# Norm and turn of a gated delta rule's outputs, chunk by chunk, in a one-core decoder layer

## The chip, the cores and the metric

The kernel runs on one core of a Trainium2 chip. A core has a matrix engine (TensorE, PE in the profile), a vector engine (VectorE, DVE), an activation engine (ScalarE, ACT), a general engine (GpSimd, POOL) and a queue from which most transfers are issued (SyncE, SP). Each works through its own instructions in order, and semaphores make one wait for another. The metric is the time of one execution in device microseconds; lower is better. Several runs are taken, and one further execution is profiled.

## What is computed

One layer of a hybrid decoder over 1024 tokens of width 1024, in float32. Four heads of a gated DeltaNet and eight heads of dilated attention share one input and one output projection; a gated MLP with a short convolution follows. The part that matters here:

```python
def step(state, xs):                       # one chunk of the delta rule, head by head
    uv, wk, qd, at, ke, ge = xs
    u = uv - wk @ state
    o = qd @ state + at @ u
    state = ge * state + ke.T @ u
    return state, o
...
o_a = gated_delta_rule(qa, ka, va, g, beta)
o_a = rmsnorm(o_a, gdn_norm_w) * silu(z)   # per head: over its 128 features, then gated
...
x = x + concat(o_a, o_b) @ w_out           # o_b: dilated attention (softmax)
h = rmsnorm(x, norm2_w)
u = causal_dwconv(h @ w_up, ffn_conv_w)
x = x + (silu(gate) * up) @ w_down
```

## The kernel before

All products run on PE. Large ones are split in a high and a low part (`whi`, `wlo` for weights, `xhi`, `xlo` for the input) and done as three products of 128 by 512 (`mm3`); a product of 128 by 512 takes one issue slot of about 0.23 us. Nearly every instruction is recorded through a helper, so the profile shows line L193 for products, L140 for other instructions and L142 for those with high priority; tiles tell them apart.

The order on PE is written by a class called `Weave`. Generators (streams) for the dense projection, for the preparation of each head, for the chain of each head and for attention yield the time until they can go on; `run` takes the ready stream of lowest level. `Weave` keeps an estimate of when each engine is free and each tile ready. The dense projection has the highest level number, so its products fill what is left. The other engines' instructions get their order from a scheduler that follows priorities, and each engine keeps that order on the chip.

The stretch in question is the **chain**. For each of four heads and eight chunks of 128 tokens, `chain` issues:

- product of the keys `kT` with the state `ct`; DVE forms the residual `r` from it;
- product of the triangular inverse (called `um` in the trace) with `r`; DVE scales it to `wke`, ACT copies it to `w`;
- product of `ktok` with `wke`; DVE adds it to the decayed state, `ct`;
- two output products with `qat` (queries and attention weights), `ct` and `w`; ACT copies the second scaled by `rq` to `vtok`, DVE adds the first;
- ACT squares the chunk of `vtok` into `osq` and sums each row into a column of `ms` (an activation, and an instruction that reads the accumulator).

When a head's eight chunks are done, DVE turns `ms` into a mean, POOL raises it to the power −0.5 (`rsqrt`, one instruction for eight columns) and multiplies the whole of `vtok` (128 by 1024) by it. A stream `finish` turns the head with four 32-by-32 block transposes on DVE into a tile `ft` and stores it in device memory (`mixer[h]`, 512 KB). `ft` takes its buffer in the ring `kT*` of large tiles. Later the dense columns of kind `z` read it back as `og` and gate it.

Beside the chain, the dense stream works through `DENSE`, a list of columns of 128 features. For each, `weight` splits the next column's weights on ACT (`whi`) and DVE (`wlo`), 1024 elements per partition in one instruction each, and DVE evicts the products of each half (for attention's columns as `aqkv`). Attention begins behind the chain: scores, a DVE pass that masks and takes the maximum (`mx`), exponentials on ACT (`sm`), a reciprocal and a scaling on DVE, and transposes on PE (`ident,sm`).

ACT needs a table for its functions. The last SiLU before the chain is that of the values of head 3 (`vT`); the next exponential is that of the first softmax. Among POOL's other work in this stretch are memsets of `pb` tiles for attention. `mark` is a one-column constant tile, and the ring `t2` has two small buffers in all, which `w1` of the merges before the chain and `oT` of attention also use.

Of the kernel before, what the change touches and what calls it, by code (L numbers as in the profile page):

```python
# [15 lines left out]
P = 128  # L16
S = 1024
KT = 8
# [23 lines left out]
FSLACK = 0.5  # L42
DENSE = ([("k", 3), ("a", 0, 0), ("a", 0, 1)] + [(c, h) for h in range(4) for c in "qv"] + [("a", 0, 2)]
         + [("a", p, i) for p in (1, 2, 3) for i in range(3)] + [("z", h) for h in range(4)])


class Weave:
# [98 lines left out]
def hybrid_layer(tc, I, out):  # L146
# [72 lines left out]

    lows_made = []  # L220

    def weight(src, n=1024, st=None):
        if st is None:
            st = raw_weight(src, n)
        hi = tile_(wp, [P, n], F32R, "whi", "whi", 2)
        lo = tile_(wp, [P, n], F32R, "wlo", "wlo", 2)
        lows_made.append(split(st, hi, lo))
        return hi, lo

    def wk(src, st=None):  # L230
        return [t.rearrange("p (k m) -> p k m", k=KT) for t in weight(src, st=st)]

    n1 = const("n1", [P, KT])
    sa.dma_start(n1, I["n1"])
# [5 lines left out]
    def rsqrt(dst, src, n):  # L240
        po_.tensor_tensor(dst, src, mhalf[:, :n], op=OP.pow)
# [221 lines left out]
    def conv_silu(xr, j, name, tag):  # L463
        y = A(name, tag)
        ac.activation(y, xr, AF.Copy, scale=gcw[:, j, 3:4])
        for d in (1, 2, 3):
            inst = ve.scalar_tensor_tensor(y[:, d:], xr[:, :S - d], gcw[:, j, 3 - d:4 - d], y[:, d:],
                                           op0=OP.mult, op1=OP.add)
            if j // 4 == 1 and d == 2 and klast:
                after(inst, klast[-1], "the keys before go first")  # L470
        if j // 4 != 1:
            ac.activation(y, y, AF.Silu)
            return y

        th = ac.activation(xr, y, AF.Tanh, scale=0.5)
        klast.append(ve.scalar_tensor_tensor(y, xr, 1.0, y, op0=OP.add, op1=OP.mult))
        kends[j - 4] = th, klast[-1]
        return y
# [35 lines left out]
    def dense():  # L514

        yield from wv.until("first")
        yield from wv.until("norms")
        wv.add(2, first_keys())

        raw = [raw_weight(I["wi"][0])]  # L520
        nxt = wk(None, raw.pop())
        raw.append(raw_weight(I["wi"][1]))
        for i, col in enumerate(DENSE):
            kind, h = col[:2]
            if kind == "z":
                yield from wv.until(("o", h))
            w = nxt
            if i + 1 < len(DENSE):
                nxt = wk(None, raw.pop())
            if i + 2 < len(DENSE):  # L530
                raw.append(raw_weight(I["wi"][i + 2]))
            pair = []
            for hh in range(2):
                pt = bank("hf")
                yield wv.need(pt, *w)
                for k in range(KT):
                    mm3(pt, [t[:, k, :] for t in w], [t[:, half(hh)] for t in xs[k]], k == 0, k == KT - 1)
                    yield 0.0

                pair.append(pt)  # L540
                if hh == 0:
                    while put_off:
                        gate(*put_off.pop(0))
                    xr = A("aqkv" if kind == "a" else "xr", "go" if kind == "k" else "ev")
                if kind == "z":
                    ve.tensor_tensor(by_row(xr)[:, :, 4 * hh:4 * hh + 4], by_token(pt), by_token(rstdB[:, half(hh)]), op=OP.mult)
                else:
                    scaled(pair, "xr", kind == "a", t=xr, hs=(hh,))
            if kind == "k":
                T["k", h] = conv_silu(xr, 4 + h, "kT", "kT*")  # L550
                wv.add(3, kprep(h))
            elif kind == "q":
                q = conv_silu(xr, h, "qT", "qa")
                wv.add(4, qprep(h, q))
            elif kind == "v":
                v = conv_silu(xr, 8 + h, "vT", "qa")
                wv.add(4, vprep(h, v))
            elif kind == "z":
                og = gated[h] = A("og", "kT*")
                for b in range(4):  # L560
                    sq_.dma_start(og[32 * b:32 * b + 32].rearrange("j (a y) -> j a y", a=4),
                                 mixer[h].rearrange("(a j) (b y) -> b j a y", a=4, b=4)[b])
                if i + 1 < len(DENSE):
                    put_off.append((og, xr))
                else:
                    gate(og, xr)
            else:
                if col[2] < 2:
                    sy.dma_start(apark[h, col[2]], xr)
                else:  # L570
                    t = A("avt", "ev")
                    ve.transpose(t.rearrange("p (c n j) -> p n c j", c=4, n=NCH), by_block(xr))
                    for b in range(4):
                        sq_.dma_start(avdram[h].rearrange("u x (b j) -> b u x j", b=4)[b],
                                     t[32 * b:32 * b + 32].rearrange("u (x j) -> u x j", j=32))
                wv.done.add(col)
        wv.done.add("dense")
# [232 lines left out]
    def chain(h):  # L810
# [14 lines left out]
        for c in range(NCH):  # L825
            cs = slice(c * P, (c + 1) * P)
            if c == 2 and h < 2:
                qb = chain_load(h, 1)
            if c == 3 and h >= 2:
                yield from wv.until(("c", h - 2, 3))  # L830
                qb = chain_load(h, 1)
            if c == 4:
                qa = qb
            qT, at = [qa[:, i, (c % 4) * P:(c % 4 + 1) * P] for i in range(2)]
            if c == 0:
                r = vtok[:, cs]
# [12 lines left out]
            ua.activation(w, ps[:, P:2 * P], AF.Copy)  # L849
            if c < NCH - 1:  # L850
                yield wv.need(wke, slack=HOP)
                mm(ps[:, 2 * P:3 * P], ktok[:, cs], wke, 0.215)
                sn = sts[:, c % 2, :]
                if c == 0:
                    uv.tensor_copy(sn, ps[:, 2 * P:3 * P])
                else:
                    uv.scalar_tensor_tensor(sn, st, ge[:, c:c + 1], ps[:, 2 * P:3 * P], op0=OP.mult, op1=OP.add)
            yield wv.need(w, qa, slack=HOP)
            po = yield from next_bank("atr")
            if c:  # L860
                mm(po[:, P:2 * P], qT, st, 0.215)
            mm(po[:, :P], at, w, 0.215)

            ua.activation(vtok[:, cs], po[:, :P], AF.Copy, scale=rq[:, c:c + 1])
            if c:
                uv.scalar_tensor_tensor(vtok[:, cs], po[:, P:2 * P], gq[:, c:c + 1], vtok[:, cs], op0=OP.mult,
                                        op1=OP.add)
            if c < NCH - 1:
                st = sn
            osq = tile_(sp, [P, P], F32, "osq", "osq", 1)  # L870
            ua.activation(osq, vtok[:, cs], AF.Square, accum_out=ms[:, c:c + 1])
            wv.done.add(("c", h, c))

        uv.tensor_scalar(ms, ms, 1.0 / 128, EPS, op0=OP.mult, op1=OP.add)
        rsqrt(ms, ms, NCH)
        po_.tensor_tensor(v8(vtok), v8(vtok), ms[:, :, None].to_broadcast([P, NCH, P]), op=OP.mult)
        wv.add(1, finish(h, vtok))

    def finish(h, osb):
        yield wv.need(osb, slack=FSLACK)  # L880
        t = A("ft", "kT*")
        by_feature, src = t.rearrange("p (b c i) -> p b c i", b=4, c=NCH), osb.rearrange("p (c b j) -> p b c j", c=NCH, b=4)
        for b in range(4):
            ve.transpose(by_feature[:, b], src[:, b])
            yield 0.4
        sy.dma_start(mixer[h], t)
        wv.done.add(("o", h))


# [882 lines left out]
```

## Time and profile before

| | |
|---|---|
| Median of 3 runs | 1201.64 us (1201.17 to 1201.66) |
| Profiled execution, its own time | 1199.71 us |
| Its span (first to last instruction) | 1197.9 us |
| Granted TensorE clock over the span | 0.998 |
| Stretch of the chain in the span | about 225 to 292 us |
| First softmax | about 293 to 298 us |

Lines of a timeline give start and duration in us, engine, line, operation, output tile, input tiles, shapes and, in brackets, how long the engine sat idle before it and what released it. Lines of a group give busy time, mean duration in ns, and idle time before. Lines of waits give who waited for whom: total us, number of times, longest us. Lines of transfers give a count, a size and the median us from issue to landing. In a table of stretches each engine has its busy us and, in brackets, its number of instructions, in the order PE, PE's weight loads, DVE, ACT, POOL; the granted clock, the transfers' share and GB/s follow. DVE, ACT and PE pipeline, so the next instruction can start before the one before it has ended.

### The profile page before, as it was taken

How to read it: one execution, taken by the hardware profiler on the slowest of the kernel's cores; microseconds unless marked ns; L12 is line 12 of the kernel's file. 1: busy time of each engine (PE TensorE's matmuls, PEld its weight loads, DVE VectorE, ACT ScalarE, POOL GpSimd, SP SyncE). 2: the span in 40 equal slices, each digit the busy share in tenths (PEclk: the TensorE clock that was granted, in tenths of full speed). 3: DMA queues.
4: the chain of work that ended last, by engine and by line, in shares of the span. 5: the costliest groups of instructions: out<-in, count | busy, mean ns of one | idle time of the engine just before them, and what ended most of it. 6: DMA issues, size and time to landing. Idle time of an engine off the chain costs nothing.

```text
span 1197.9 us, 18219 instructions
## 1 busy us (share of the span) xinstructions
PE 1184.3 (99%) x6994; PEld 979.5 (82%) x6994; DVE 967.5 (81%) x1552; ACT 566.4 (47%) x1113; POOL 54.3 (5%) x50
## 2 busy tenths in 40 slices
PE   9999999998999999999999999999999999999997
PEld 7888888897777777888888888888888888888887
DVE  7686985586766687777898888989888889898987
ACT  7383344363433344555454544445444453445452
POOL 0212110023000000000000000000000000000001
PEclk9999999999999999999999999999999999999999
DMA  7423235536643314443222223131222396356724
GB/s 237 106 75 103 78 118 131 150 114 189 185 100 128 98 37 142 148 158 106 77 70 99 88 71 106 53 106 59 100 89 69 105 378 211 119 181 218 240 99 155
DMA packets 98600, 152.72 MB, mean 127 GB/s; under 512 B 37936, under 2 KB 51024, under 8 KB 98512
## 3 DMA queue, kind: packets, MB, share of 16 engines
q1 hardware_dynamic: 97792, 151.02, 39.4%
q8 instruction: 55, 0.90, 0.3%
q10 hardware_dynamic: 720, 0.53, 0.1%
q14 instruction: 33, 0.27, 0.1%
HBM read 115.59 MB, written 35.93 MB: 126 GB/s over the span
## 4 chain that ended last, share of the span: by engine, by line
PE 95%; DVE 2%; ACT 1%; issue 1%; DMA 1%; POOL 0%; DVEq 0%; ACTq 0%; POOLq 0%
PE ps L193 46%; PE pa L193 20%; PE dw L193 17%; PE pc L193 10%; PE ps L197 1%; PE ps L202 1%; DMA wst<-in_wu 1%; ACT sm L142 0%; PE warm L193 0%; DVE x1h L140 0%; DVE sm L142 0%; DVE aqkv L140 0%; DVE T L140 0%; ACT L142 0%; DVE wst L140 0%
## 5 line engine op out<-in xcount | busy, mean ns | idle before, releaser
L193 PE MATMUL dw<-pr 128*128 128x512 f32 (+1 forms) x984 | 211.4, 376 | 0.0
L193 PEld LDWEIGHTS dw<-pr 128*128 128x128 f32 x984 | 176.7, 188 | 33.7
L193 PE MATMUL ps<-xhi,whi 128*128 128x512 f32 x448 | 184.4, 412 | 0.0
L193 PE MATMUL ps<-xhi,wlo 128*128 128x512 f32 x448 | 175.2, 391 | 0.0
L193 PE MATMUL ps<-xlo,whi 128*128 128x512 f32 x448 | 174.8, 390 | 0.0
L193 PE MATMUL pa<-T,pair 128*128 128x512 f32 x528 | 127.1, 390 | 0.5 <-ACT u L140 0.5
L193 PEld LDWEIGHTS pa<-T,pair 128*128 128x128 f32 x528 | 98.9, 188 | 21.5 <-ACT u L140 1.0
L193 PEld LDWEIGHTS ps<-xhi,whi 128*128 128x128 f32 x448 | 84.3, 188 | 19.3 <-issue 2.7
L193 PEld LDWEIGHTS ps<-xhi,wlo 128*128 128x128 f32 x448 | 84.1, 188 | 18.5
L193 PEld LDWEIGHTS ps<-xlo,whi 128*128 128x128 f32 x448 | 84.4, 188 | 14.3
L140 ACT ACTIVATE u<-pa 128x512 f32<-128x512 f32 x44 | 26.3, 598 | 109.7 <-PE pa L193 109.7
L140 DVE SCALAR_TENSOR_TENSOR y<-xu,fcw,y 128x1023 f32<-128x1023 f32 (+1 forms) x44 | 56.4, 1281 | 24.4 <-ACT y L140 24.4
L140 ACT ACTIVATE whi<-wst 128x1024 fp32r<-128x1024 f32 (+2 forms) x38 | 38.5, 1014 | 68.8 <-PE ps L193 61.6
L140 ACT ACTIVATE pr<-wd 128x1024 fp32r<-128x1024 f32 x33 | 35.0, 1061 | 74.6 <-DVE wd L140 37.2
L193 PE MATMUL pa<-B,A 128*128 128x512 f32 x264 | 63.5, 389 | 0.0
L193 PE MATMUL pa<-T,S 128*128 128x512 f32 x264 | 63.4, 389 | 0.0
L193 PE MATMUL pc<-T,S 128*128 128x512 f32 x264 | 63.4, 389 | 0.0
L193 PE MATMUL pc<-B,pair 128*128 128x512 f32 x264 | 63.4, 389 | 0.0
L140 DVE TENSOR_TENSOR wst<-wst 128x512 f32<-128x512 f32 x88 | 60.4, 686 | 0.8
L193 PE MATMUL ps<-B,pair 128*128 128x512 f32 x252 | 60.5, 389 | 0.0
L142 ACT ACTIVATE sm<-sm,mx 128x128 f32<-128x128 f32 (+7 forms) x64 | 35.5, 555 | 50.3 <-DVE mx L142 50.3
L193 PEld LDWEIGHTS pc<-T,S 128*128 128x128 f32 x264 | 49.5, 188 | 10.3
(242 smaller groups left out, 2234.2 us busy)
## 6 DMA issues: line engine op xcount, KB each, us to landing
wst<-in_wu SPq DMA_DIRECT2D x44, 512.0 KB, 3.6
wd<-in_wd SPq DMA_DIRECT2D x44, 512.0 KB, 4.5
wst<-in_wi SPq DMA_DIRECT2D x25, 512.0 KB, 3.6
upark<-y SPq DMA_DIRECT2D x22, 512.0 KB, 3.5
r<-upark SPq DMA_DIRECT2D x22, 512.0 KB, 10.1
wa<-in_wd SPq DMA_DIRECT2D x22, 256.0 KB, 2.9
apark<-aqkv SPq DMA_DIRECT2D x8, 512.0 KB, 2.7
wst<-in_wo SPq DMA_DIRECT2D x8, 512.0 KB, 3.8
```

The lines of the kernel that those rows point to most:

```text
L140: return getattr(eng, op)(*a, **kw)
L142: return getattr(eng, op)(*a, **kw)
L193: tc.stamp_issue_order_token(nc.tensor.matmul(dst, lhs, rhs, start=start, stop=stop, **kw).ins, TOKEN)
L197: tc.stamp_issue_order_token(nc.tensor.transpose(dst, src, ident).ins, TOKEN)
L202: tc.stamp_issue_order_token(nc.tensor.transpose(dst, src[rows], ident[rows, rows]).ins, TOKEN)
```

## The change

- The mean square comes out of the square itself (a scale of 128^−0.5). Behind each chunk's square POOL adds the epsilon and takes the power for that one column.
- ACT multiplies each chunk by its column (`normed`), one chunk behind; the large multiply on POOL and the late instruction on DVE are gone.
- Two halves of a head are turned apart (`half_turned`), the first behind chunk 4, the second in `finish`, each with two transposes and a store of 256 KB of its own, in packets of 512 bytes. The half tiles are in the ring `t2`.
- The weights of three dense columns (`CHAINED`) are split in two halves of 512.
- One exponential of a column is ordered behind the last SiLU, and writes `mark`.

```diff
+CHAINED = [("a", 1, 1), ("a", 1, 2), ("a", 2, 0)]
...
-    def weight(src, n=1024, st=None):
+    def weight(src, n=1024, st=None, parts=1):
...
-        lows_made.append(split(st, hi, lo))
+        for i in range(parts):
+            sl = slice(i * n // parts, (i + 1) * n // parts)
+            low = split(st[:, sl], hi[:, sl], lo[:, sl])
+        lows_made.append(low)
...
-            ac.activation(y, y, AF.Silu)
+            last["silu"] = ac.activation(y, y, AF.Silu)
...
-                nxt = wk(None, raw.pop())
+                nxt = wk(None, raw.pop(), 1 + (DENSE[i + 1] in CHAINED))
...
                 v = conv_silu(xr, 8 + h, "vT", "qa")
+                if h == H - 1:
+                    after(ac.activation(mark, mhalf[:, :1], AF.Exp), last["silu"], "the table changes once")
...
-            ua.activation(osq, vtok[:, cs], AF.Square, accum_out=ms[:, c:c + 1])
+            ua.activation(osq, vtok[:, cs], AF.Square, scale=128.0 ** -0.5, accum_out=ms[:, c:c + 1])
+            po_.tensor_scalar(ms[:, c:c + 1], ms[:, c:c + 1], EPS, None, op0=OP.add)
+            rsqrt(ms[:, c:c + 1], ms[:, c:c + 1], 1)
+            if c:
+                normed(vtok, ms, c - 1)
+            if c == 4:
+                half_turned(h, vtok, 0)
             wv.done.add(("c", h, c))
 
-        uv.tensor_scalar(ms, ms, 1.0 / 128, EPS, op0=OP.mult, op1=OP.add)
-        rsqrt(ms, ms, NCH)
-        po_.tensor_tensor(v8(vtok), v8(vtok), ms[:, :, None].to_broadcast([P, NCH, P]), op=OP.mult)
-        wv.add(1, finish(h, vtok))
-
-    def finish(h, osb):
-        yield wv.need(osb, slack=FSLACK)
-        t = A("ft", "kT*")
-        by_feature, src = t.rearrange("p (b c i) -> p b c i", b=4, c=NCH), osb.rearrange("p (c b j) -> p b c j", c=NCH, b=4)
-        for b in range(4):
-            ve.transpose(by_feature[:, b], src[:, b])
-            yield 0.4
-        sy.dma_start(mixer[h], t)
+        wv.add(1, finish(h, vtok, ms))
+
+    def normed(osb, ms, c):
+        cs = slice(c * P, (c + 1) * P)
+        wv.free["scalar"] = max(wv.free["scalar"], wv.pe) + 0.23
+        nc.scalar.activation(osb[:, cs], osb[:, cs], AF.Copy, scale=ms[:, c:c + 1])
+
+    def half_turned(h, osb, hh):
+        t = tile_(sp, [P, 512], F32, "ft", "t2", 2)
+        by_feature = t.rearrange("p (b c i) -> p c b i", b=4, c=4)
+        src = osb[:, half(hh)].rearrange("p (c b j) -> p c b j", c=4, b=4)
+        for c in (0, 2):
+            wv.free["vector"] = max(wv.free["vector"], wv.pe) + 0.34
+            nc.vector.transpose(by_feature[:, c:c + 2], src[:, c:c + 2])
+        sy.dma_start(mixer[h].rearrange("p (b c i) -> p b c i", b=4, c=NCH)[:, :, 4 * hh:4 * hh + 4],
+                     t.rearrange("p (b c i) -> p b c i", b=4, c=4))
+
+    def finish(h, osb, ms):
+        yield wv.need(ms, slack=FSLACK)
+        normed(osb, ms, NCH - 1)
+        half_turned(h, osb, 1)
         wv.done.add(("o", h))
```

More of the change, by code (lines that the diff above doesn't have):

```diff
@@ L226, in weight, with wk @@
         lo = tile_(wp, [P, n], F32R, "wlo", "wlo", 2)
-        lows_made.append(split(st, hi, lo))
+        for i in range(parts):
+            sl = slice(i * n // parts, (i + 1) * n // parts)
+            low = split(st[:, sl], hi[:, sl], lo[:, sl])
+        lows_made.append(low)
         return hi, lo
-    def wk(src, st=None):
-        return [t.rearrange("p (k m) -> p k m", k=KT) for t in weight(src, st=st)]
+    def wk(src, st=None, parts=1):
+        return [t.rearrange("p (k m) -> p k m", k=KT) for t in weight(src, st=st, parts=parts)]
     n1 = const("n1", [P, KT])
```

## The prediction

> **What bounds the kernel now.** I read the engines' busy time first, then who waited for whom on TensorE (PE), and then, stretch by stretch, the part of the trace that the change touches.
>
> ```profile
> PE 1184.3 (99%) x6994; PEld 979.5 (82%) x6994; DVE 967.5 (81%) x1552; ACT 566.4 (47%) x1113; POOL 54.3 (5%) x50
> ...
> PE ps L193 <- DVE ct L142: 1.6, 2, 1.2
> PE ps L193 <- ACT w L142: 1.4, 2, 1.0
> ...
> PE ps L202 <- DVE sm L142: 1.1, 1, 1.1
> ```
>
> PE is busy 99% of the span. The change adds and removes no product, so it can move the end only through PE's waits. The list of waits (total us, times, longest) has 1.6 + 1.4 + 1.1 = 4.1 us that end in the chain or in the softmax behind it. That is all that can be won there.
>
> ```profile
> 235.00:245.00 10.00, 9.58 (x75) 8.99 (x75) 7.63 (x25) 6.32 (x27) 0.00 (x0) 1.00 0.01 2
> 245.00:255.00 10.00, 10.00 (x83) 9.72 (x82) 8.46 (x30) 7.02 (x32) 0.53 (x1) 1.00 0.31 105
> ...
> 265.00:275.00 10.00, 7.83 (x49) 6.52 (x48) 9.21 (x22) 4.41 (x15) 6.27 (x5) 1.00 0.69 237
> ```
>
> These are three stretches of the chain (busy us of PE, PE's weight loads, VectorE (DVE), ScalarE (ACT) and GpSimd (POOL) in 10 us). In 265:275 PE loses 2.17 us while POOL is busy 6.27 us and DVE 9.21. From 235 to 255 PE is nearly full, but DVE (7.6 and 8.5) and ACT (6.3 and 7.0) are close to it. So there is a hole to fill late and little room in the middle.
>
> **The hole at 269.** Two timelines, merged:
>
> ```profile
> 266.88 0.96 DVE L142 TENSOR_SCALAR ms<-ms 128x8 f32<-128x8 f32 x1 [0.27 <-ACT osq L142]
> 267.57 1.06 ACT L140 ACTIVATE whi<-wst 128x1024 fp32r<-128x1024 f32 x1
> 268.67 1.06 DVE L140 TENSOR_TENSOR aqkv<-ps,rstdB 128x512 f32<-128x512 f32 x1
> 269.56 0.41 DVE L140 STREAM_TRANSPOSE ft<-vtok 128x256 f32<-128x256 f32 x1
> 269.64 1.90 POOL L140 TENSOR_TENSOR vtok<-vtok,ms 128x1024 f32<-128x1024 f32 x1
> 269.90 0.32 DVE L142 TENSOR_SCALAR wke<-ps,ke 128x128 f32<-128x128 f32 x1
> 270.25 0.28 ACT L142 ACTIVATE w<-ps 128x128 f32<-128x128 f32 x1 [1.33 <-DVE wke L142]
> 270.38 2.23 DVE L140 TENSOR_TENSOR wlo<-wst,whi 128x1024 fp32r<-128x1024 f32 x1
> 270.58 0.49 PE L193 MATMUL ps<-wke,ktok 128*128 128x128 f32 x2 [0.98 <-ACT w L142]
> 272.54 0.33 DVE L142 SCALAR_TENSOR_TENSOR ct<-ct,ge,ps 128x128 f32<-128x128 f32 x1
> 272.93 0.49 PE L193 MATMUL ps<-ct,kT 128*128 128x128 f32 x2 [1.19 <-DVE ct L142]
> ...
> L140 DVE TENSOR_TENSOR wlo<-wst,whi x25: 1183/1220/2233, 63.0 to 458.4; 128x1024 fp32r<-128x1024 f32 x25
> ```
>
> DVE works in order: the eviction aqkv and a transpose stand ahead of wke, ACT's w follows wke, and the state product follows w (PE's 0.98 us gap). Then the weight split wlo, median 1.22 us, takes 2.23 beside POOL's 1.90 us multiply, and ct behind it brings the 1.19 us gap. The change takes away POOL's multiply and the late ms instruction (0.96 us), and cuts wlo in two with ct between the halves in the built order. What stays late is the eviction (1.06) and one transpose (0.41). The second gap can go wholly, 1.19 us (or, if ct comes behind both halves, only the 1.01 us that POOL cost): I take 1.1. Of the first, 0 to 0.98, about half stays, since the eviction does: I take 0.5. Together 1.6 of 2.17.
>
> The Trainium skill (SBUF — State Buffer, section "Who interferes with whom") says that a DVE instruction with two SBUF inputs and a GpSimd instruction that reads SBUF exclude each other for the whole instruction. The trace agrees: 2.23 us is 1.22 and 1.01 more, under the multiply's 1.90. By that rule the small POOL instructions that come instead could hold up the six weight halves alone, the one kind with two SBUF inputs here, by one power each; if a third of 6 × 0.54 us reached PE, the sum would come out 1.1 us later.
>
> **The table.**
>
> ```profile
> 196.99 1.06 ACT L140 ACTIVATE vT<-vT 128x1024 f32<-128x1024 f32 x1 [3.65 <-DVE vT L140]
> 199.38 0.59 ACT L140 ACTIVATE w<-ps 32x512 f32<-32x512 f32 x1 [1.33 <-PE ps L193]
> ...
> 293.31 1.28 ACT L142 ACT_TABLE_LOAD   x1 [1.00 <-DVE mx L142]
> 294.61 0.40 ACT L142 ACTIVATE sm<-sm,mx 128x128 f32<-128x128 f32 x1
> ...
> 295.52 0.17 DVE L142 RECIPROCAL mx<-mx 128x2 f32<-128x2 f32 x1 [1.37 <-ACT sm L142]
> ...
> 297.90 0.60 PE L202 MATMUL ps<-ident,sm 64*128 64x64 f32 x8 [1.08 <-DVE sm L142]
> ```
>
> The first softmax waits for the exponential's table, 1.28 us, and PE for the softmax, 1.08. The one-element exponential moves the load behind the last SiLU, which ends at 198.05; ACT then idles 1.33 us. The load fits, and the exponential behind it makes w late by some 0.2 us. w is awaited by the second merge products, which in the built order stand behind 18 dense products of 0.23 us: that is the cover, and without it the move would cost the 0.2. In the built program no second load appears before the softmax. What is next late there: one normed copy of head 3 and one transpose now stand among the exponentials and ahead of the reciprocal. I take 1.0 of 1.08.
>
> The Trainium skill (ScalarE: Activation LUTs, "What ACT_TABLE_LOAD costs") gives 1283 ns for the load and 1380 more for a drain, 2.66 in all. The trace has the 1.28 and the exponential 0.02 us behind it, no drain; by the page the move would be worth 1.38 us more, but PE's gap is only 1.08.
>
> **What is added.** 32 normed copies on ACT, 32 additions and 32 powers of one column on POOL, in place of 4 powers of eight columns and 4 multiplies; the 16 transposes stay, half of them earlier; 8 stores of half a head in place of 4.
>
> ```profile
> L140 POOL TENSOR_TENSOR ms<-ms,mhalf 128x8 f32<-128x8 f32 x4 | 6.5, 1636 | 11.7 <-DVE ms L142 11.6
> L140 POOL TENSOR_TENSOR rs<-rs,mhalf 128x2 f32<-128x2 f32 x2 | 1.4, 696 | 20.4 <-DVE rs L140 20.4
> L140 POOL COPY mark<-x 1x1 f32<-1x1 f32 x1 | 0.2, 178 | 12.7 <-DVE x L140 12.7
> ...
> 237.49 0.31 ACT L142 ACTIVATE osq<-vtok 128x128 f32<-128x128 f32 x1
> 237.70 0.19 ACT L142 ACTIVATION_READ_ACCUMULATOR osq<-vtok 128x1 f32 x1
> 237.80 0.35 ACT L142 ACTIVATE vtok<-ps,rq 128x128 f32<-128x128 f32 x1
> 238.04 0.27 ACT L142 ACTIVATE w<-ps 128x128 f32<-128x128 f32 x1
> 238.20 0.31 ACT L142 ACTIVATE osq<-vtok 128x128 f32<-128x128 f32 x1
> ...
> L140 DVE STREAM_TRANSPOSE ft<-vtok 128x256 f32<-128x256 f32 x16 | 6.0, 418 | 0.9 <-POOL vtok L140 0.9
> ```
>
> A power costs 0.70 us for 2 columns and 1.64 for 8, so by that line (696 − 1 × 157 ns) 0.54 for one. The addition on POOL isn't in the trace: between the 0.18 of a one-element copy and the power's 0.54; I take 0.18, the nearest in size. With hand-overs of 0.05 to 0.15 the norm of a chunk is ready 0.9 to 1.3 us behind its accumulator. A normed copy occupies ACT 0.24 us (237.80 to 238.04, the copy with a scale). In the built order 2 to 4 ACT instructions, 0.16 to 0.24 us each, stand between a square and its normed copy, so ACT will sometimes stand still for it, and w queues behind. w has little room: in the hole above ACT gave it at 270.53 and PE began at 270.58. Eight transposes, 0.42 each, come into 239 to 259, 3.3 us more for a DVE that is 76 to 85% busy. The halves of three weights add three instructions on ACT and on DVE, about 0.2 us of fixed time each (ACT: 0.31 us for 128 elements, 1.06 for 1024), in idle time that both have late in the chain. Against that, two groups of three dense products (0.7 us each) stand earlier among the chain's products and give it room. How much of this lands on PE the trace doesn't show: from 0 to 20 copies × 0.35 us of standing still = 7 us (the 59 ACT instructions of 235 to 255 are four per chunk, so 15 chunks in 20 us, 20 by 261). I take 0.6, near the low end: in 10 us ACT idles 3.0 to 3.7 and gets 8 × 0.24 = 1.9 more; DVE idles 1.5 to 2.4 and gets 1.7.
>
> On SP the eight stores issue before the loads of the weights and of attention's avdram tiles that stood ahead of them, some 0.35 to 0.6 us each; these loads have over 10 us before their use. The reads of og still follow the last store, and only the gates behind the last dense columns want them.
>
> **The sum.** 1.6 + 1.0 − 0.6 = 2.0 us. The profiled execution took 1199.71 us (span 1197.9 and 1.8 around it); it becomes 1197.7. The median of the runs, 1201.64, lies 1.93 above the profiled one, so I forecast 1199.6. A difference of 0.2%, 2.4 us, is what I take a measurement to tell from none.
>
> **Rivals.** *All of it is won.* The normed copies and transposes lie in idle time, and all 4.1 us of the waits go: 1197.5. For it: the earlier dense products. Against it: two gaps are left whose causes stay, an eviction ahead of ct and w's late turn.
>
> ```profile
> 239.74 0.49 PE L193 MATMUL ps<-ct,kT 128*128 128x128 f32 x2 [0.42 <-DVE ct L142]
> ...
> 257.51 0.49 PE L193 MATMUL ps<-wke,ktok 128*128 128x128 f32 x2 [0.47 <-ACT w L142]
> ```
>
> *The half tiles hold DVE up.* ft now has two buffers in all, so a transpose into one waits until its last store has landed.
>
> ```profile
> mixer<-ft SPq DMA_DIRECT2D x4, 512.0 KB, 3.4
> ...
> mixer<-oT SPq DMA_DIRECT2D x7, 256.0 KB, 2.3
> ...
> 265.87 1.85 SPq L140 DMA_DIRECT2D vc<-avdram  x3
> ```
>
> A store of 256 KB should take 2.3 to 3.4 us. Head 2's first half stands eight DVE instructions (8 × 0.33 = 2.6 us) behind the last transpose of the half it waits for: 0 to 1 us. Head 1's last half waits for head 0's, whose store stands on SP's queue behind the avdram loads, at 0.62 us each some twelve issues, 7 us: 1 to 2 us. If two thirds of these 3 us reach PE, the 2.0 are gone: 1201.6.
>
> *ACT stands still for POOL (the slower end).* POOL takes some 0.85 us per chunk (0.18 + 0.54 + hand-overs), and a chunk comes every 1.25 us (8 in 10), so norms queue; besides, pb's memsets stand between the powers in POOL's queue and wait for products of head 2. Each normed copy that comes early holds w, and the state product behind w. At 0.25 us for each of 20 copies PE loses 5.0; less the 2.6 won, 1201.64 + 2.4 = 1204.0. It decides above 2.6 / 20 = 0.13 us per copy. For it: w is used as soon as it is there. Against it: the dense products between.
>
> **How the numbers follow.** Forecast 0.44 (own range 1198.2 to 1201.3; 0.17 of it faster by over 0.2%, 0.27 within). All won 0.20, faster. Half tiles 0.13, within. ACT behind POOL 0.23, slower. So faster 0.37, within 0.2% 0.40, slower 0.23. The range goes from 1197.0, the rival that wins all and half a microsecond for restarts of PE, to 1203.9, just short of the slow rival's time; a fifth is left out.
>
> **What would show it.** In the profile after: no wait above 0.6 us near the weight split of the third chained column; no table load before the first softmax and PE's wait on sm under 0.2; POOL's powers at 0.5 to 0.6 us. The forecast is wrong if PE's waits on w or ct exceed 3 us, if ACT's normed copies wait for POOL by more than 8 us in all, or if ft's transposes wait for stores.

## The result and the profile after

| | before | after |
|---|---|---|
| Median of 20 runs each | 1201.68 us | 1203.57 us (1202.35 to 1205.97) |
| Ratio, 95% interval | | 1.0016 (1.0009 to 1.0023) |
| Profiled execution, its span | 1199.71, 1197.9 us | 1204.29, 1202.4 us |
| First product of the chain to first product of the output projection, in the span | 225.5 to 465.6: 240.1 us | 226.1 to 470.3: 244.2 us |

The changed kernel is slower by 1.9 us where 2.0 us less were forecast. The last row is the ruler of the sections below: the change works between these two products, and the start of a run, which varies by up to 1.3 us in these profiles, is left out. By the ruler the change costs 4.1 us in its profiled execution. Taken again beside other kernels, the changed kernel's ratio was 1.0040 (1.0026 to 1.0054) and the ruler showed 244.9.

The first part of the page of the changed kernel, busy time, share and instructions of each engine:

```profile
PE 1187.3 (99%) x6994; PEld 981.6 (82%) x6994; DVE 966.3 (80%) x1551; ACT 576.8 (48%) x1149; POOL 65.6 (5%) x106
```

The products are the same 6994, and PE is busy 3 us longer for them. The list of waits on PE (total us, times, longest):

```profile
PE ps L196 <- ACT w L145: 3.5, 3, 3.1
PE ps L196 <- DVE vtok L145: 2.1, 1, 2.1
...
PE ps L196 <- DVE ct L145: 0.4, 1, 0.4
```

The wait on `ct` (1.6 before) has shrunk and that on `sm` (1.1 before) has gone, as forecast. Two single waits of 3.1 and 2.1 us stand in their place. The timeline around the first:

```profile
263.84 1.09 DVE L143 TENSOR_TENSOR aqkv<-ps,rstdB 128x512 f32<-128x512 f32 x1 [0.35 <-PE ps L196]
264.76 0.32 DVE L145 SCALAR_TENSOR_TENSOR ct<-ct,ge,ps 128x128 f32<-128x128 f32 x1
...
265.28 0.45 DVE L901 STREAM_TRANSPOSE ft<-vtok 128x256 f32<-128x256 f32 x1 [0.20 <-DMA mixer<-ft]
...
265.65 0.65 DVE L143 TENSOR_TENSOR wlo<-wst,whi 128x512 fp32r<-128x512 f32 x1
266.22 0.34 DVE L145 SCALAR_TENSOR_TENSOR ct<-ct,ge,ps 128x128 f32<-128x128 f32 x1
266.47 0.69 DVE L143 TENSOR_TENSOR wlo<-wst,whi 128x512 fp32r<-128x512 f32 x1
267.07 0.60 DVE L145 SCALAR_TENSOR_TENSOR vtok<-ps,gq,vtok 128x128 f32<-128x128 f32 x2
...
267.47 0.49 PE L196 MATMUL ps<-ct,qat 128*128 128x128 f32 x2 [2.11 <-DVE vtok L145]
```

DVE is not idle for long here: it works through an eviction, a transpose and two weight halves while PE waits for the `vtok` that stands behind them. The second wait is of another kind:

```profile
273.10 1.95 SPq L143 DMA_DIRECT2D mixer<-ft  x2
...
275.96 0.39 PE L196 MATMUL ps<-w,qat 128*128 128x128 f32 x2
278.08 0.77 DVE L901 STREAM_TRANSPOSE ft<-vtok 128x256 f32<-128x256 f32 x2 [3.38 <-DMA mixer<-ft]
...
278.77 0.31 DVE L145 TENSOR_SCALAR wke<-ps,ke 128x128 f32<-128x128 f32 x1
...
279.11 0.28 ACT L145 ACTIVATE w<-ps 128x128 f32<-128x128 f32 x1 [3.21 <-DVE wke L145]
...
279.44 0.59 PE L196 MATMUL ps<-wke,ktok 128*128 128x128 f32 x2 [3.10 <-ACT w L145]
```

Read it upwards. PE waits 3.10 us for `w`, ACT 3.21 for `wke`, and DVE, which would make `wke`, stands 3.38 us before a transpose into a half tile whose store has not landed. The list names ACT; the cause is two links further up. The chain of work that ended last has the store as one piece of 4.95 us:

```profile
273.10 4.95 DMA mixer<-ft
```

And behind that wait PE runs at half its clock. Stretches of 1 us with PE's busy us, its instructions and the granted clock:

```profile
278.00:279.00 1.00, 0.00 (x0) 1.00 0.03 8
279.00:280.00 1.00, 0.56 (x3) 0.85 0.60 182
280.00:281.00 1.00, 1.00 (x7) 0.50 0.97 272
281.00:282.00 1.00, 1.00 (x6) 0.50 0.97 280
282.00:283.00 1.00, 1.00 (x4) 0.50 0.28 72
283.00:284.00 1.00, 1.00 (x7) 0.95 0.42 124
```

The clock lost in these rows is 0.15 + 3 × 0.50 + 0.05 = 1.70 us. It is an estimate: the part of full speed that was missing, summed over the rows. It is in no list of waits, since PE counts as busy.

### The profile page after: what moved, and what is told of

Its sections match the earlier page's. It is cut to its first block, busy times and chain, and to the rows that moved or that the text cites. A ratio compares the mean times of both kernels' runs of the same rounds, so it can differ in the third digit from the quotient of the medians.

```text
span 1202.4 us, 18334 instructions
## 1 busy us (share of the span) xinstructions
PE 1187.3 (99%) x6994; PEld 981.6 (82%) x6994; DVE 966.3 (80%) x1551; ACT 576.8 (48%) x1149; POOL 65.6 (5%) x106
## 4 chain that ended last, share of the span: by engine, by line
PE 95%; DVE 2%; DMA 1%; ACT 1%; issue 0%; POOL 0%; DVEq 0%; ACTq 0%; POOLq 0%
PE ps L196 46%; PE pa L196 20%; PE dw L196 17%; PE pc L196 10%; PE ps L200 1%; PE ps L205 1%; DMA mixer<-ft 1%; DMA wst<-in_wu 0%; ACT sm L145 0%; PE warm L196 0%; DVE sm L145 0%; DVE x1h L143 0%; DVE aqkv L143 0%; DVE ft L901 0%; DVE T L143 0%
## 5 line engine op out<-in xcount | busy, mean ns | idle before, releaser
L143 ACT ACTIVATE whi<-wst 128x1024 fp32r<-128x1024 f32 (+3 forms) x41 | 38.8, 954 | 70.2 <-PE ps L196 63.4
L196 PEld LDWEIGHTS pa<-T,S 128*128 128x128 f32 x264 | 49.5, 188 | 10.3
```

Source lines behind the costliest of these rows:

```text
L143: return getattr(eng, op)(*a, **kw)
L196: tc.stamp_issue_order_token(nc.tensor.matmul(dst, lhs, rhs, start=start, stop=stop, **kw).ins, TOKEN)
```

## The experiments

Every ratio is to runs of the kernel before that were taken beside the run on the same chip; the ruler is read from one profiled execution of each kernel. The kernel before has 240.1 us on it. The last two columns split the ruler further: how long PE stands idle within it, and the clock lost in it, worked out as above from rows of 1 us. PE does the same 2194 products between the two marks in every kernel. TensorE's products come in the order of the changed kernel in `own_buffer`, `no_halves`, `no_power`, `no_copies` and `no_turn`, in that of the kernel before in `table_alone`, `halves_alone` and the two `no_multiply`; the others have orders of their own.

| kernel | what it is | ratio to before (95%) | ruler, us | PE idle in it, us | clock lost in it, us |
|---|---|---|---|---|---|
| before | | 1 | 240.1 | 4.4 | none |
| after | the change | 1.0016 (1.0009 to 1.0023) | 244.2 | 6.3 | 1.7 |
| after, again | | 1.0040 (1.0026 to 1.0054) | 244.9 | 7.4 | 1.7 |
| own_buffer | after, the second half tile of heads 1 and 3 out of the ring | 1.0007 (0.9998 to 1.0015) | 240.9 | 4.1 | none |
| no_halves | after, weights whole | 1.0032 (1.0019 to 1.0044) | 244.1 | 6.3 | 1.7 |
| whole_head | after, heads turned whole | 1.0034 (1.0022 to 1.0047) | 244.6 | 5.5 | 1.7 |
| table_alone | before, early exponential | 0.9998 (0.9989 to 1.0006) | 240.0 | 4.4 | none |
| halves_alone | before, weights in halves | 0.9999 (0.9988 to 1.0009) | 240.1 | 4.5 | none |
| no_multiply | before without GpSimd's multiply | 0.9976 (0.9966 to 0.9986) | 237.3 | 1.7 | none |
| no_multiply_table | the same, early exponential | 0.9972 (0.9962 to 0.9982) | 237.3 | 1.6 | none |
| no_power | own_buffer without add and power | 1.0011 (1.0003 to 1.0020) | 240.9 | 4.3 | none |
| no_copies | own_buffer without add, power, copies | 1.0000 (0.9992 to 1.0009) | 241.1 | 3.2 | 1.7 |
| no_turn | after without transposes | 0.9986 (0.9977 to 0.9994) | 239.0 | 2.7 | none |
| later_half | own_buffer, first half a chunk later | 1.0003 (0.9995 to 1.0012) | 241.2 | 4.9 | none |
| mixed_turn | heads 0, 1 whole, 2, 3 in halves | 0.9991 (0.9983 to 1.0000) | 240.0 | 2.3 | none |
| vector_multiply | before, multiply on VectorE | 1.0017 (1.0007 to 1.0027) | 242.9 | 5.4 | 1.7 |
| scalar_copies | before, multiply on ScalarE | 0.9983 (0.9974 to 0.9991) | 238.6 | 2.9 | none |
| copies_table_halves | the same, with table and halves | 0.9989 (0.9980 to 0.9999) | 240.0 | 2.9 | 1.7 |

**The changed kernel again.** 

> The changed kernel itself, so that the others of this call stand beside it on one chip. From the first comparison (ratio 1.0016 to the kernel before): 1.9 us above the kernel before, within 1.1 to 2.8. In its profile: a stall of TensorE over 3 us near 276 and a granted clock of 0.50 for some 3 us behind it again; if that is chance and not the ring, one of the two is missing.

The ratio was 1.0040, above the range expected; a wait of 3.6 us on `w` stood near 276 again, and the clock fell behind it. So the stall is no chance of one execution.

**The ring.**

```diff
-        t = tile_(sp, [P, 512], F32, "ft", "t2", 2)
+        t = tile_(sp, [P, 512], F32, "ft", *(("ft", 1) if h % 2 and hh else ("t2", 2)))
```

> The changed kernel, but the second half tile of the odd heads lies in a buffer of its own instead of the ring of two; the order of TensorE's instructions stays the same. Theory A (the ring holds VectorE up): the 3.38 us for which VectorE stood before the transposes of head 1's second half goes, with it TensorE's stall of 3.26 us near 276, and some of the slow instructions behind it (up to 1.7 us): 1198.6 to 1200.3 us against 1203.6 of the changed kernel. Rival B (ScalarE stands still for GpSimd's small steps): the stall is only handed to the next wait, 1203.0 to 1203.8. Rival C (the work that was added to the engines, no wait): 1203.3 to 1203.8.

The ratio falls to 1.0007. PE's waits, then the stretch from 276 to 284 of both kernels, changed kernel second:

```profile
PE ps L196 <- DVE vtok L145: 2.5, 1, 2.5
...
PE ps L196 <- ACT w L145: 0.7, 3, 0.4
```

```profile
276.00:284.00 8.00, 7.92 (x50) 6.82 (x50) 5.13 (x14) 4.18 (x15) 2.57 (x7) 1.00 0.80 238
```

```profile
276.00:284.00 8.00, 4.90 (x23) 4.30 (x22) 3.18 (x10) 2.40 (x9) 1.58 (x4) 0.79 0.65 193
```

The 3.1 us wait is gone, and with it the loss of clock: 50 instructions of PE where the changed kernel does 23. The ruler falls by 3.3 us, to 240.9. The wait and the clock were 3.10 + 1.70 = 4.8 us; other waits take part of it back (`vtok` near 265 0.4 longer, one of 0.37 near 273). Theory A holds for this stall. Its time is not reached: the kernel is 0.8 us above the kernel before, where 1.4 to 3.1 below were expected. The wait on `vtok` stays, at 2.5 us (2.1 in the changed kernel, 2.7 when it was taken again).

**Whole heads.** `finish` turns a head with four transposes into a tile of `kT*` and one store, as before; the rest is the change.

> The changed kernel, but each head is turned whole after its last chunk, as in the kernel before, into a tile of the big ring, with four transposes and one store; chunks are still normed one by one, weights still halved, the exponential still early. Theory A: both stalls that the transposes' place brings (2.28 near 265 and 3.26 near 276) go, the hole near 269 and the table's 1.0 stay won: 1198.5 to 1200.5 us. Rival B (ScalarE stands still for GpSimd): 1203 or more, since every normed copy still waits for its power. Rival C (added work): 1202.5 to 1203.5.

It is no faster than the change: 244.6 on the ruler. The stalls in the chain did go (PE's waits on `w` and `vtok` are 0.6 and 0.3 us), but the transposes came back before the first softmax:

```profile
300.35 1.42 DVE L143 STREAM_TRANSPOSE ft<-vtok 128x256 f32<-128x256 f32 x4
...
301.74 1.07 DVE L143 TENSOR_TENSOR aqkv<-ps,rstdB 128x512 f32<-128x512 f32 x1
...
303.03 1.22 DVE L143 TENSOR_TENSOR wlo<-wst,whi 128x1024 fp32r<-128x1024 f32 x1
304.16 0.16 DVE L145 RECIPROCAL mx<-mx 128x2 f32<-128x2 f32 x1
...
304.62 0.61 DVE L145 TENSOR_SCALAR sm<-sm,mx 128x256 f32<-128x256 f32 x2
...
305.02 0.60 PE L205 MATMUL ps<-ident,sm 64*128 64x64 f32 x8 [1.58 <-DVE sm L145]
```

DVE does 3.7 us of other work before the softmax is scaled, and the granted clock is 0.62 and 0.53 from 306 to 310. The order of products differs here from both kernels, so the run prices this kernel, and the place of the transposes only as read in these rows. The time lies where rival B had put it (1203 or more), but in these rows PE waits behind VectorE's transposes, eviction and weight, and `no_power` below speaks against rival B.

**The exponential alone, and the multiply.** The first adds the exponential behind the last SiLU to the kernel before. The other two take GpSimd's `tensor_tensor` on `vtok` out of the kernel before, keeping its cost in `Weave`'s books so that the order stays.

> The kernel before with only the exponential behind the last SiLU; TensorE's order is the same as before. If the table's load stood on the path: 1.0 us less than before, 1200.7 us. Rival (the wait before the first softmax is given back at the next wait): 1201.4 to 1201.8, no change.

> The kernel before without GpSimd's multiply of 128x1024 (the four heads' outputs stay unnormed, so that part of the computation is left out); TensorE's order is the same as before, the table's load stays before the first softmax. If VectorE is slow beside that multiply (2.23 us for the weight's low part against 1.22): the wait of 0.97 us near 269 goes, the one of 1.19 us behind it may go too, 1.0 to 2.2 us less than before; the wait before the first softmax stays, since the table's load holds the exponential. Rival (the late scaling is what counts, not the multiply): no change, within 0.4 us.

> As the one without the multiply, and the exponential behind the last SiLU besides. The table alone brought nothing (ratio 0.9998), and its trace shows VectorE's two scalings of the first softmax at 2.04 us beside GpSimd's multiply, where the kernel before has 0.77 us. If the two hide each other: with the multiply gone the table's 1.0 to 1.1 us now count, 1.0 us less than the kernel without the multiply alone and 2.0 to 3.3 us less than before. Rival (the table's load is covered by other work in any case): the same as without the multiply, within 0.3 us.

The exponential alone brings nothing: 0.9998, and PE's wait before the first softmax is still 1.1 us. Its timeline says why; two rows of the kernel before stand ahead of it for comparison:

```profile
294.31 1.90 POOL L140 TENSOR_TENSOR vtok<-vtok,ms 128x1024 f32<-128x1024 f32 x1
...
295.73 0.77 DVE L142 TENSOR_SCALAR sm<-sm,mx 128x128 f32<-128x128 f32 x2
```

```profile
293.33 0.40 ACT L142 ACTIVATE sm<-sm,mx 128x128 f32<-128x128 f32 x1 [1.02 <-DVE mx L142]
...
294.32 1.90 POOL L140 TENSOR_TENSOR vtok<-vtok,ms 128x1024 f32<-128x1024 f32 x1
294.45 2.04 DVE L142 TENSOR_SCALAR sm<-sm,mx 128x128 f32<-128x128 f32 x2
```

The load is gone and the exponential runs 1.28 us earlier than before. The two scalings behind it now fall under the whole of GpSimd's multiply, take 2.04 us instead of 0.77, and end when they did before. What PE waits for comes behind them on DVE. The expected 1.0 us was wrong: the rival holds.

Without the multiply the waits on `w` and `ct` shrink from 1.4 and 1.6 us, and `sm` is off the list, which the expectation had not foreseen:

```profile
PE ps L193 <- ACT w L142: 0.7, 2, 0.5
PE ps L193 <- DVE ct L142: 0.6, 2, 0.4
```

The ruler falls by 2.8 us, more than the 1.0 to 2.2 expected, and the early exponential adds nothing to that (237.3 both times, and the ratios' intervals overlap almost wholly). Two rows of the kernel without the multiply show how:

```profile
270.02 1.20 DVE L140 TENSOR_TENSOR wlo<-wst,whi 128x1024 fp32r<-128x1024 f32 x1
...
291.33 1.28 ACT L142 ACT_TABLE_LOAD   x1
```

The weight's low part takes 1.20 us where it took 2.23. The table load comes 2 us earlier than before, ahead of the wait for the maximum, and is over at 292.61, when the first maximum comes, so that it holds nothing up. The late `ms` on VectorE, which the prediction lists with 0.96 us as work of its own, is no work of that length either: it began under GpSimd's first multiply (265.45 to 267.35), and in the kernel without it it takes 0.13 us. More than the contention goes with the multiply: VectorE's transposes need not wait for it, and the order on VectorE shifts. All three waits hang on the multiply; how much of the 2.8 us is its time beside VectorE, and how much the order, these runs do not part.

The Trainium skill (SBUF — State Buffer, "Who interferes with whom") lists `tensor_scalar` among the operations that can enter a two-port mode and then contend with GpSimd. The 2.04 us agree; the prediction had named the weight halves as the one kind that could.

**The halves of the weights.**

> The kernel before with only the three weights split in halves; TensorE's order is the same as before. The prediction's step (a chained step passes between two halves, each shorter beside GpSimd's multiply than the 2.23 us of the whole): 0.5 to 1.0 us less than before. Rival (the multiply holds VectorE for its own 1.90 us, whatever the piece): no change, within 0.4 us.

> The changed kernel with the three weights split whole again (no entry in the list); TensorE's order is that of the changed kernel. Prediction's step (halves let a chained step pass between them): 0.3 to 0.7 us more, 1203.9 to 1204.3. Theory A (the weight is not what VectorE waits with): 1203.4 to 1203.8, no change. Rival D (two halves of 0.65 and 0.69 in place of one of 1.22 only add work): 0.1 to 0.7 us less, 1202.9 to 1203.5.

Added to the kernel before they bring nothing (0.9999, ruler 240.1), and taken from the changed kernel they move the ruler by 0.1 (244.1). The prediction's step on the halves found no support, and the rivals that saw no change hold.

**ScalarE behind GpSimd.** `no_power` leaves out the two lines on `po_` and `rsqrt`, `no_copies` the `normed` activation as well; their costs stay in the books.

> The changed kernel with the buffer of its own for the odd heads' second half, and without GpSimd's addition and power for each chunk (chunks are scaled by the raw mean square, so that part of the computation is left out); TensorE's order is that of the changed kernel. Rival B (ScalarE stands still for GpSimd, 8.0 us of waits in 18 places in the changed kernel): 1.0 to 3.0 us less than with the buffer of its own, so below the kernel before. Theory A (those waits are slack, what is left sits in VectorE's order near 265): the same as with the buffer of its own, 0.4 to 1.2 us above the kernel before.

> The changed kernel with the buffer of its own, without GpSimd's addition and power for each chunk and without ScalarE's normed copies (the outputs stay unnormed, so that part of the computation is left out); TensorE's order is that of the changed kernel. If the copies on ScalarE eat the gain: 2 to 3 us less than before, a ratio near 0.998, and the 271 pairs of chained products fall from 33.05 to about 31.6 us. If the order of the products and VectorE's transposes do: at most 1 us less than with the own buffer, ratio 0.9995 to 1.001, and the pairs stay near 33 us.

Both stay level with the own buffer: 240.9 and 241.1 on the ruler. In the changed kernel, and with the own buffer, ACT waited 8.0 us for POOL in 18 places, and taking these steps out won nothing: the wait on `vtok` fell from 2.5 to 0.9 us, but those on `w` and `ct` rose from 0.7 and 0.4 to 2.2 and 0.8. Rival B falls. For the 12.8 us of copies on ACT the answer is less sure. The ratio, 1.0000, is within the noise of 1.0007, and the expected 2 to 3 us did not come; but this profile lost 1.7 us of clock that the own buffer kept, and without that loss the ruler would read 239.4, 1.5 us less. Up to that much may be the copies'. Without the copies the stall near 265 is as it was, 2.3 us, and this time the clock fell behind it:

```profile
PE ps L196 <- DVE vtok L145: 2.3, 1, 2.3
```

```profile
268.00:269.00 1.00, 1.00 (x7) 0.74 0.70 220
269.00:270.00 1.00, 1.00 (x4) 0.50 0.38 112
270.00:271.00 1.00, 1.00 (x5) 0.50 0.70 150
```

**The transposes.** In `no_turn` each half is stored straight from `vtok`; the order of products is that of the change. In `later_half` the first half is turned at `c == 5`.

> The changed kernel without the 16 transposes on VectorE: the halves are stored straight from the normed outputs (the outputs stay unturned, so that part of the computation is left out); copies, powers, halved weights and early exponential stay, and TensorE's order is that of the changed kernel. If the transposes in VectorE's queue make the stall near 265: the wait of 2.1 to 2.7 us there falls under 1.2 us, the one near 276 goes with the ring, and the kernel is 1.0 to 2.5 us less than before. If the stall is made by the scaling of 1.0 us and the weight's two halves: at least 1.5 us of it stays, and the kernel is within 1.0 us of before.

> The changed kernel with the buffer of its own, the first half of each head turned after chunk 5 instead of chunk 4 (16 rows of TensorE's order move). If the transposes of 0.45 us in VectorE's queue make the stall of 2.5 us near 265: it shrinks by 0.9 us (two transposes) or goes, 0.5 to 2.0 us less than with the own buffer. Rival (the two weight halves and the 1.03 us scaling of the product ahead of it make it, the transposes only share the queue): within 0.5 us of the own buffer.

Without transposes the wait on `vtok` falls from 2.5 to 1.5 us and the one near 276 does not come back:

```profile
PE ps L196 <- DVE vtok L145: 1.5, 1, 1.5
```

The ruler is 239.0, 1.9 us below the own buffer. So the turned halves cost more than the one wait in the ring. The 1.9 us are not the transposes' own time alone: with the own buffer they still stood 5.3 us for normed copies and 0.6 for stores in DVE's queue, and `no_turn` takes all of that away at once. Each of the two expectations came half true: the time fell as the first said, and the 1.5 us of the wait that the second gave to the scaling (the eviction) and the weight's halves stayed. One chunk later brings no gain: the wait on `vtok` is 1.9 us, one of 1.65 us on `ct` appears near 278, and the ruler shows 241.2. That second wait is the ring again, although it has the extra buffer:

```profile
279.08 0.45 DVE L901 STREAM_TRANSPOSE ft<-vtok 128x256 f32<-128x256 f32 x1 [2.57 <-DMA mixer<-ft]
...
279.81 0.75 PE L196 MATMUL ps<-ct,kT 128*128 128x128 f32 x4 [1.65 <-DVE ct L145]
```

So the run does not tell what the place of the transposes is worth by itself.

**Where else the multiply can go.** `mixed_turn` turns heads 0 and 1 whole and heads 2 and 3 in halves. In the other two `finish` waits for `ms` instead of `vtok` and multiplies ahead of its transposes:

```diff
+        for i in range(2):
...
+            ve.tensor_tensor(v8(osb)[:, 4 * i:4 * i + 4], v8(osb)[:, 4 * i:4 * i + 4],
+                             ms[:, 4 * i:4 * i + 4, None].to_broadcast([P, 4, P]), op=OP.mult)
```

in `vector_multiply`, and in `scalar_copies`

```diff
+        for c in range(NCH):
+            ac.activation(osb[:, c * P:(c + 1) * P], osb[:, c * P:(c + 1) * P], AF.Copy, scale=ms[:, c:c + 1])
```

> The changed kernel with heads 0 and 1 turned whole after the last chunk in the big ring, heads 2 and 3 turned in halves, the last half of head 3 in a buffer of its own. In the kernel that turned all heads whole, TensorE stood 2.54 us between 225 and 305, against 3.80 with halves and the own buffer, and then lost 1.9 us before the first softmax behind four transposes of 1.42 us, and some 1.5 us to a halved clock. Theory A (place of the transposes decides): both are avoided, 1200.0 to 1201.5 us where the kernel before has 1200.2. Rival C (norming chunk by chunk costs by itself, through the order that it brings): 1202.5 us or more.

> The kernel before with GpSimd's multiply of 128x1024 done by VectorE, as two of 128x512 ahead of the transposes; TensorE's order is that of before but for 6 rows. Without the multiply the kernel ran at a ratio of 0.9976 (2.7 us less). If that was VectorE standing beside GpSimd: most of it is kept, less the added VectorE work where it is on the path (two of about 0.6 us a head, at the worst both heads of the last pair): 0.3 to 2.7 us less than before. Rival (VectorE bounds this stretch): 0.5 to 2.5 us more than before.

> The kernel before with GpSimd's multiply done by ScalarE, as eight scaled copies of 128x128 a head (0.40 us each in the changed kernel) after the head's last chunk; TensorE's order is that of before but for 6 rows. If VectorE beside GpSimd was the cost and ScalarE has room: 1.0 to 2.7 us less than before. Rival (ScalarE's copies hold up the chained w and the first softmax's exponentials: 8 by 0.40 us for two heads at once): no gain, or up to 3 us more than before.

> The kernel before with GpSimd's multiply done by ScalarE's eight scaled copies a head (ratio 0.9983 alone), and the change's other two parts besides: the exponential behind the last SiLU and the three weights in halves. Each of the two brought nothing alone (0.9998 and 0.9999). If they were covered by the multiply: the wait of 1.15 us near 271 behind the whole weight (1.21 us) shrinks by 0.5, 0.3 to 0.8 us less than the copies alone, a ratio of 0.9976 to 0.9981. Rival (they are off the path in any case): 0.9983 again, within 0.0003.

`mixed_turn` reaches a ratio of 0.9991 and 240.0 us on the ruler: rival C (1202.5 or more) falls, so norming chunk by chunk need not make the kernel slower. Its waits are nearly gone, PE's idle time is 2.3 us where the kernel before has 4.4, and yet the ruler is no shorter, because PE is busy 237.7 us for the same products where before it was 235.7.

On DVE the multiply makes the ruler 2.8 us longer than before, as the rival said. Two pieces stand among the softmax's work, PE waits 2.05 us, and its clock halves, which is 1.7 of the 2.8. A part of the timeline, and the stretches with the columns as above:

```profile
297.37 0.67 DVE L140 TENSOR_TENSOR vtok<-vtok,ms 128x512 f32<-128x512 f32 x1
...
299.46 0.28 PE L202 MATMUL ps<-ident,sm 64*128 64x64 f32 x2 [2.05 <-DVE sm L142]
```

```profile
299.00:300.00 1.00, 0.54 (x8) 0.95 1.06 212
300.00:301.00 1.00, 1.00 (x4) 0.50 1.14 232
301.00:302.00 1.00, 1.00 (x4) 0.50 1.13 246
```

On ACT it is the best kernel that does the whole computation, 1198.64 us against 1201.46, a ratio of 0.9983 (0.9974 to 0.9991), faster than both kernels compared here. Its waits:

```profile
PE ps L193 <- DVE ct L142: 1.6, 2, 1.1
...
PE ps L193 <- ACT w L142: 1.0, 2, 0.5
```

The wait on `sm` is off the list and `w` is down from 1.4; `ct` is not, since the four transposes (1.42 us) and the whole weight (1.21 us) stand ahead of it on DVE. Adding the table and the halves took none of that away (waits of 1.6 and 1.1) and came out at 0.9989; in that profile the clock fell to 0.50 from 274 to 277, behind waits of 0.59 and 1.14 us that the copies alone have too (0.51 and 1.15), at a clock of 1.00. Without those 1.7 us of clock its ruler would read 238.3, level with the copies alone, so the rival that puts both parts off the path holds.

## Why the prediction was wrong

- **The bound.** That PE's waits of 4.1 us in the chain and the softmax are all that can be won was right as a ceiling: the best removal won 2.8 of them. That the change can move the end "only through PE's waits" was not. Of the 4.1 us by which the ruler grew, PE's idle time is 1.9; the other 2.2 are time in which PE is busy for longer with the same products, 1.7 of them the lost clock.
- **The hole at 269.** The cause was right, and the 1.6 us was close: without the multiply the waits on `w` and `ct` fall by 0.7 and 1.0 us. The halves' share in it was wrong: none. The late `ms` was not a second cause: its 0.96 us became 0.13 with the multiply gone.
- **The table.** "I take 1.0 of 1.08" failed, in its cause. The load and PE's wait stood in one fence and I took the one for the cause of the other; GpSimd's multiply from 294.31, beside the scalings between them, I left out. With the load gone the scalings ran into the multiply. In the changed kernel the wait did go (off the list of waits), but there the multiply is gone as well, and without the multiply the load is covered anyway. So the 1.0 us came out nearly right by luck: it was won by the term beside it.
- **What is added.** The estimates of size were fair for POOL: a power 0.57 us (0.54 forecast), an addition 0.22 (0.18). A normed copy takes 0.40, where I had 0.24 from one start to the next. That this work lies beside other work held for POOL; for ACT's copies it is open. It failed for DVE: I let eight earlier transposes fit in its idle time, and the 16 with their waits are worth 1.9 us (all left out). With the own buffer two of them stand with an eviction and a weight ahead of one `vtok` that PE needs. I had summed idle time over 10 us, and the queue in front of one instruction is what counts. So the 0.6 us of the sum became 3.6: these 1.9, and 1.7 for the rest of the change.
- **The half tiles.** This rival had the right place and the right chain: "Head 1's last half waits for head 0's, whose store stands on SP's queue behind the avdram loads". But the sum had no term for it. As a rival it was priced at 1 to 2 us, and the wait was 3.38. I reckoned with a landing in 2.3 to 3.4 us, and the store took 4.95 from its issue. Above all I had no term for what follows a wait of 3 us: the clock at 0.50, 1.70 us more. With these two numbers the rival comes out at 1199.6 + 3.10 + 1.70 = 1204.4, on the slow side, where I had it within 0.2%. On the ruler the ring costs 3.3 us. With enough buffers the kernel is still not faster than before (1.0007, 0.9998 to 1.0015), so it is this step together with the one above that turned 2.0 us less into 4.1 more on the ruler: 3.3 for the ring, 3.0 more than forecast for what is added, 0.2 more than forecast won.
- **ACT behind POOL.** The rival that I gave the slower end fell. The waits were larger than it had them (8.0 us in 18 places, for 5.0 in 20), and the kernel without the powers behind them was no faster. That the time came out near its 1204.0 is luck.
- **The signs.** Those of being wrong did their work: PE's waits on `w` were 3.5 us (over 3), the transposes waited 3.6 us for stores, and a wait of 2.11 us stood beside the weight's halves (over 0.6). Those of the table and of the powers came as named, which alone would have looked like success.

Along the ruler the kernels make a path: 240.1 before, 237.3 without the multiply, 239.0 with all of the change but its transposes, 240.9 with these and enough buffers, 244.2 with the ring of two. So the multiply gives 2.8 us, the ring with its clock takes 3.3, the transposes 1.9, and the rest of the change 1.7. Of these 1.7, idle time of PE is 1.1, which goes with the wait of 1.5 us that `no_turn` keeps near 265, where an eviction and a weight stand ahead of `vtok`. The other 0.6 us PE is busy for longer. At full clock it is busy 235.6 to 235.7 us of the ruler in the kernels that have the order of before, and, with the lost clock taken off, 235.8 to 236.8 in those with the changed order and 237.4 to 237.7 in `whole_head` and `mixed_turn`. So a part of the price is in busy time, which no list of waits shows; what makes the same products take longer stays open. That the order makes the wait of 1.5 us, and not something else that these kernels share, was not separated either.

The path rests on one execution of each kernel. By the ratios, each against its own runs of the kernel before, the same four steps are 2.9, 1.1 to 4.0, 2.5 and 1.2 us. The sizes are good to about 1 us, and the ring's is the least certain.

## To carry to other kernels

When a large tile is cut to be handed on earlier, count its buffers against the time from the issue of a store to its landing, and look who stands in the queue behind the instruction that refills the buffer. Where two things stand side by side ahead of a wait, take each away in turn before pricing either: here the one gave all of the gain and the other nothing. Price a new wait of some 1.5 us or more on TensorE with the 1.7 us of clock that it may lose behind it, which no list of waits shows.

## What was unexpected of the hardware

The granted clock fell to 0.50 for about 3.4 us after waits of TensorE of 3.57 us (the changed kernel again), of 3.10 us, of 2.3 us (`no_copies`), of 2.05 us (`vector_multiply`), and of 1.58 us shortly after one of 0.38 (`whole_head`). It did not after 2.48 us (`own_buffer`), nor after 1.9 and 1.65 (`later_half`) nor after 1.51 (`no_turn`). So length alone does not decide, and nearly the same waits (0.5 to 0.6, then 1.14 or 1.15 us) lost it in `copies_table_halves` and not in `scalar_copies`. Each time the loss came to 1.7 us.

The Trainium skill (TensorE: Matmul & The Clock Gate, "HAM oscillation — how this bites in real kernels") asks for no idle gaps over about 3.4 us. All but one of the waits that lost the clock here are shorter than that, and the measurement decides. The Trainium skill (TensorE: Matmul & The Clock Gate, "What's actually happening") tells of a window of 3413 ns that runs free of the kernel. The length of the loss agrees with that window. A free-running window would explain that one wait loses the clock and a longer one does not, but no run here shows where the window lay.

A store of 256 KB in packets of 512 bytes took 2.6 to 5.5 us from issue to landing in the changed kernel (median 3.0), and the one that mattered took 4.95.
